# Two of the four block sums of a seven-product group move from VectorE to accumulating DMAs, and blocks take any free slot

## The chip, the cores and the metric

The kernel runs on one core of one Trainium2 chip. The metric is device time in microseconds (us) of one execution; the number for a kernel is the median of several runs. A profile is one more execution, recorded by the hardware profiler; its span runs from the first to the last instruction of the program.

## The reference, cut to what matters

One pre-norm decoder layer on 256 tokens of width 2048, with four token mixers side by side. Nearly all of the work is in products of 256 rows with wide float32 weights:

```python
h = rms_norm(x, norm_w)                      # 256 x 2048
p = h @ w_in                                 # 2048 x (z 2048, gates 8192, q/k/v of four mixers, indexer)
branches = (o_dsa, o_fox, o_diff, o_dil)     # four attentions, 4 heads of 128 each
for b in range(4):
    y = branches[b] * silu(z_parts[b])
    term = sigmoid(g_parts[b]) * (y @ w_branch[b])
    merged = term if merged is None else merged + term
out = rms_norm(x + merged @ w_out, final_norm_w)
```

## The kernel before

**Blocks, splits and products.** Weights come from HBM in blocks of 512 rows by 512 columns (1 MB, tile `raw`, 128 partitions x 2048 floats), each by one DMA of the SP queue. A block is cut in two halves of 128x1024. ScalarE copies each half to a rounded high part (`whi`, line 194), VectorE subtracts to get the low part (`wlo`, line 207), and TensorE multiplies in three passes: activation high by `whi`, activation low by `whi`, activation high by `wlo` (`three`, lines 365 to 367). There are 8 buffers for `whi` and 6 for `wlo`.

**Units.** The program is a list of units, each with one block and its matmuls. The main loop writes, for each half of each unit: the `wlo` split that lies 5 halves ahead, the `whi` split that lies 7 halves ahead, and then the matmuls of this half. What evicts a PSUM bank (`post`) is written after the unit's matmuls. The order of each engine's queue is the order in which this loop writes instructions; every engine works its queue in order and waits on semaphores.

**A group (`seven`).** A product of 256 tokens by 2048 rows by 1024 columns is a group of eleven units. For half of the rows the 2x2 blocks B11, B12, B21, B22 and the two halves of the tokens are combined so that seven products (P1 to P7, 12 matmuls each) take the place of eight. The other half of the rows goes through four plain units (c2a, c2b, c1a, c1b, 24 matmuls each). Four PSUM banks (X, Y, Z, W) collect. The seven products need four sums of blocks; before, all four are VectorE additions of whole blocks in place (`plus`, line 174). There are 17 groups: two (`ps_qk`, `ps_zv`) and two for the gates (`ps_g`) for each of the four mixers, and one for `w_out`. The usual order is P5 P1 P3 c2a P6 c2b P7 P2 c1a P4 c1b; the first group and the last one use another, written under `late`. P5 leaves its product in bank W. It is read from there (`p5`, by ScalarE), and c2a goes on adding to the same bank: for each half c2a has 6 matmuls to bank Z and then 6 to bank W.

**Slots.** There are six slots for `raw`. Before, each block has a fixed slot (0 to 3 for the B blocks, 4 and 5 for the others), and the next block of a slot is loaded when the last `wlo` split of the one before has been written.

**Threads.** Attention, the indexer and other small work are Python generators. A round of all active ones is written between units whenever a count of unit costs passes `pace`.

Of the kernel before, what the change touches and what calls it, by code (L numbers as in the profile page):

```python
# [20 lines left out]
KC = D // P  # L21
# [52 lines left out]
class Raw:  # L74


    def __init__(self, slot, src, k0, nk, c0, n):
        self.slot, self.src, self.k0, self.nk, self.c0, self.n = slot, src, k0, nk, c0, n
        self.tile = self.then = None
# [31 lines left out]
def body(ctx: ExitStack, tc, x, norm_w, w_in, fox_b_f, lq1, lk1, lq2, lk2, subln_w,  # L111
# [37 lines left out]
    waiting = [deque() for _ in range(SLOTS)]  # L149

    def load(r, parts=1, part=None):
        if not part:
            r.tile = wp.tile([P, 2048], F32, name="raw", tag=f"raw{r.slot}", bufs=1)
# [185 lines left out]
    def tok_units(src, c0, act, slots, evict, name, need=(), start=()):  # L339
# [3 lines left out]
        nk = 4 * len(slots)  # L343
        for i, slot in enumerate(slots):
# [5 lines left out]
            units.append(Unit(Raw(slot, src, 4 * i, 4, c0, 512), mm))  # L350
# [27 lines left out]
    def T_units(c0, evict, name, slots, ps_of=main_ps):  # L378
# [3 lines left out]
        for k0 in range(0, KC, 4):  # L382
# [11 lines left out]
            units.append(Unit(Raw(slots[k0 // 4], w_in, k0, 4, c0, 512), mm))  # L394
# [40 lines left out]
    def seven(src, c1, c2, base, ev, name, need={}, start=(), late=False, s0=0):  # L435
# [5 lines left out]
        B11, B12 = Raw(0, src, s0, 4, c1, 512), Raw(1, src, s0, 4, c2, 512)  # L441
        B21, B22 = Raw(3, src, s0 + 4, 4, c1, 512), Raw(2, src, s0 + 4, 4, c2, 512)
# [30 lines left out]
        def c(k0, c0, two):  # L473
            return Unit(Raw(4 + k0 // 4 % 2, src, k0, 4, c0, 512), plain(k0, two))
# [8 lines left out]
        def unit(what, raw, mm, post=(), frees=(), loads=(), pre=()):  # L483
            u = Unit(raw, mm, frees=frees, loads=loads, post=post, pre=pre, need=need.get(what, ()))
            u.cost = 12
            return u

        u5 = unit("P5", B12, product("V" if late else "W", form(1, 4), True),
                  [read(ev.p5, "V" if late else "W")], loads=[B12, B11, B22, B21],
                  pre=[lambda: plus(B12, B11)])  # L490
        u1 = unit("P1", B11, product("Y", whole(0, s0), True), [read(ev.p1, "Y")])
        u3 = unit("P3", B22, product("Z", form(0, 4), not late))
        second = [lambda: plus(B12, B22), lambda: free([B22])]
        fourth = [lambda: plus(B21, B12), lambda: free([B12])]
        u6 = unit("P6", B12, product("Y", form(0, 0)), [read(ev.u2, "Y")])
        u7 = unit("P7", B11, product("Y", form(1, 0)), [read(ev.u3, "Y")], frees=[B11],
                  pre=[lambda: plus(B11, B12, ALU.subtract)])
        u2 = unit("P2", B21, product("X", whole(0, s0 + 4), True))
        u4 = unit("P4", B21, product("Y", whole(1, s0 + 4)), frees=[B21])
        c2a, c2b = c(p0, c2, "ZW"), c(p0 + 4, c2, "ZW")  # L500
        c1a, c1b = c(p0, c1, "XY"), c(p0 + 4, c1, "XY")
        c2a.need += need.get("c2a", ())
        c1b.need += need.get("c1b", ())
        c1b.post += [read(ev.c11, "X", True), read(ev.c21, "Y", True)]
        c1b.start += start
        if late:
            u5.after += second[:1]
            u3.after += second[1:]
            u6.after += fourth
            u1.cost = u2.cost = 24  # L510
            u7.post += [read(ev.c12, "Z", True), read(ev.c22, "W", True)]
            return [c2a, u1, u2, u5, u3, u6, c2b, u7, c1a, u4, c1b]
        u6.pre += second
        u2.after += fourth
        c2b.post += [read(ev.c12, "Z", True)]
        u2.post += [read(ev.c22, "W", True)]
        return [u5, u1, u3, c2a, u6, c2b, u7, u2, c1a, u4, c1b]

    class Tok:


        def __init__(self, dst, s1, s2, late=False):
            self.dst, self.s1, self.s2, self.late = dst, s1, s2, late

        def p1(self, ps):
            if self.late:
                self.d1, self.d2 = self.dst()
            nc.scalar.activation(self.d1[:, 0], ps, AF.Copy, scale=self.s1[:, 0:1])

        def p5(self, ps):  # L530
            if self.late:
                nc.scalar.activation(self.d2[:, 1], ps, AF.Copy, scale=self.s2[:, 1:2])
            else:
                self.d1, self.d2 = self.dst()
# [7 lines left out]
        def u3(self, ps):  # L542
            if self.late:
                nc.vector.scalar_tensor_tensor(self.d2[:, 1], ps, self.s2[:, 1:2],  # L544
                                               self.d2[:, 1], op0=ALU.mult, op1=ALU.subtract)
            else:
# [733 lines left out]
```

## Time and profile before

| | |
|---|---|
| median of 3 runs | 1005.34 us (1004.07 to 1007.09) |
| the profiled execution's own time | 1004.6 us |
| its span | 1002.8 us |
| TensorE busy, of the span | 959.9 us, 96% |
| VectorE busy | 852.9 us, 85% |
| ScalarE busy | 626.3 us, 62% |
| GpSimd busy | 50.2 us, 5% |
| mean granted TensorE clock | 0.985 |

A busy time is the union of an engine's instructions. The profiled execution took 1.8 us more than its span. A row of the view of waits names the instruction that waited, the one that released it, the total in us, how often, and the longest.

### The profile page before, as it was taken

Reading aid. Unit: us, or ns where it says so; the run is one execution under the profiler, and the core shown is the slowest. Engines: PE = TensorE matmul, PEld = TensorE weight load, DVE = VectorE, ACT = ScalarE, POOL = GpSimd, SP = SyncE. Lnnn points to the kernel's source line nnn. Section 1 sums busy time; section 2 is a strip of 40 time slices with the busy share of each in tenths; the row PEclk is TensorE's granted clock in tenths of the full one; section 3 lists DMA queues with packets and bytes.
Section 4 is the critical chain, followed back from the end, with each engine's and each line's share of the span. In section 5 each row is a group of like instructions: output and inputs, shape, how many; then the busy total and the mean of one; then the engine's idle time right before and its main releaser. Section 6 shows DMA issues by size and latency. Waiting matters only on the chain.

```text
span 1002.8 us, 12075 instructions
## 1 busy us (share of the span) xinstructions
PE 959.9 (96%) x4443; PEld 790.4 (79%) x4443; DVE 852.9 (85%) x985; ACT 626.3 (62%) x828; POOL 50.2 (5%) x67
## 2 busy tenths in 40 slices
PE   9997898999999999889999999999999999999896
PEld 8876686878888887668888887788888878888676
DVE  5898899989788987789799899887998989779982
ACT  5847464796655656685456667864666787544551
POOL 2010000000000000020100000001000000010130
PEclk9999899999999999899999999999999999999998
DMA  9936355555766555337786655577756465866232
GB/s 318 298 134 196 124 168 167 169 168 184 278 225 228 197 168 168 126 126 238 223 232 202 218 168 168 168 262 208 236 201 210 164 210 187 309 232 238 86 125 84
DMA packets 100043, 195.81 MB, mean 195 GB/s; under 512 B 7811, under 2 KB 10021, under 8 KB 99600
## 3 DMA queue, kind: packets, MB, share of 16 engines
q1 hardware_dynamic: 96240, 181.06, 53.5%
q0 software_dynamic: 3712, 13.98, 5.3%
q8 instruction: 35, 0.57, 0.2%
q14 instruction: 24, 0.20, 0.1%
q10 hardware_dynamic: 32, 0.01, 0.0%
HBM read 186.61 MB, written 8.41 MB: 194 GB/s over the span
## 4 chain that ended last, share of the span: by engine, by line
PE 78%; DVE 13%; issue 4%; ACT 3%; DMA 1%; POOL 0%; ACTq 0%; POOLq 0%; DVEq 0%; SPq 0%
PE ps_g L365 9%; PE ps_g L367 9%; PE ps_g L366 9%; DVE wlo L207 6%; PE ps_zv L367 5%; PE ps_zv L365 5%; PE ps_zv L366 5%; PE ps_qk L365 5%; PE ps_qk L366 5%; PE ps_qk L367 5%; PE ps_iq L370 3%; PE ps_b L367 3%; PE ps_b L365 3%; PE ps_b L366 3%; DVE raw L174 3%
## 5 line engine op out<-in xcount | busy, mean ns | idle before, releaser
L194 ACT ACTIVATE whi<-raw 128x1024 fp32r<-128x1024 f32 (+1 forms) x439 | 448.1, 1051 | 221.3 <-DVE raw L174 70.1
L207 DVE TENSOR_TENSOR wlo<-raw,whi 128x1024 fp32r<-128x1024 f32 (+1 forms) x439 | 523.2, 1222 | 44.6 <-ACT whi L194 9.9
L174 DVE TENSOR_TENSOR raw<-raw 128x2048 f32<-128x2048 f32 x68 | 155.6, 2288 | 19.4 <-DMA raw<-in_w_in_dram 17.9
L365 PE MATMUL ps_g<-whi,hT 128*128 128x512 f32 x352 | 141.9, 403 | 0.0
L367 PE MATMUL ps_g<-wlo,hT 128*128 128x512 f32 x352 | 138.2, 393 | 0.0
L366 PE MATMUL ps_g<-whi,hT 128*128 128x512 f32 x352 | 138.1, 392 | 0.0
L365 PEld LDWEIGHTS ps_g<-whi,hT 128*128 128x128 f32 x352 | 66.7, 189 | 15.2 <-issue 1.6
L367 PEld LDWEIGHTS ps_g<-wlo,hT 128*128 128x128 f32 x352 | 66.7, 189 | 14.4
L366 PEld LDWEIGHTS ps_g<-whi,hT 128*128 128x128 f32 x352 | 66.7, 190 | 13.3
L365 PE MATMUL ps_qk<-whi,hT 128*128 128x512 f32 x176 | 69.8, 396 | 4.4 <-DVE tok L544 4.4
L367 PE MATMUL ps_zv<-wlo,hT 128*128 128x512 f32 x176 | 69.7, 396 | 3.0 <-DVE wlo L207 3.0
L365 PE MATMUL ps_zv<-whi,hT 128*128 128x512 f32 x176 | 69.7, 396 | 0.7 <-ACT v L547 0.7
L366 PE MATMUL ps_qk<-whi,hT 128*128 128x512 f32 x176 | 69.3, 394 | 0.0
L367 PE MATMUL ps_qk<-wlo,hT 128*128 128x512 f32 x176 | 69.2, 393 | 0.0
L366 PE MATMUL ps_zv<-whi,hT 128*128 128x512 f32 x176 | 69.0, 392 | 0.0
L365 PE MATMUL ps_g<-whi,sf 128*128 128x512 f32 x128 | 52.2, 408 | 0.0
L366 PE MATMUL ps_g<-whi,sf 128*128 128x512 f32 x128 | 50.3, 393 | 0.0
L367 PE MATMUL ps_g<-wlo,sf 128*128 128x512 f32 x128 | 50.3, 393 | 0.0
L365 PE MATMUL ps_b<-whi,yT 128*128 128x512 f32 x128 | 49.8, 389 | 0.0
L367 PE MATMUL ps_b<-wlo,yT 128*128 128x512 f32 x128 | 49.8, 389 | 0.0
L366 PE MATMUL ps_b<-whi,yT 128*128 128x512 f32 x128 | 49.8, 389 | 0.0
L365 PEld LDWEIGHTS ps_qk<-whi,hT 128*128 128x128 f32 x176 | 33.6, 191 | 12.4 <-DVE tok L544 4.8
(266 smaller groups left out, 1519.9 us busy)
## 6 DMA issues: line engine op xcount, KB each, us to landing
raw<-in_w_in_dram SPq DMA_DIRECT2D x132, 1024.0 KB, 5.1
raw<-in_w_branch_dram SPq DMA_DIRECT2D x16, 1024.0 KB, 5.3
raw<-in_w_out_dram SPq DMA_DIRECT2D x16, 1024.0 KB, 5.3
md<-g POOLq DMA_DIRECT2D x12, 512.0 KB, 5.3
raw<-in_w_in_dram SPq DMA_DIRECT2D x7, 512.0 KB, 9.7
xs<-in_x_dram SPq DMA_DIRECT2D x8, 256.0 KB, 7.5
mp<-md POOLq DMA_DIRECT2D x4, 512.0 KB, 3.6
xf<-in_x_dram POOLq DMA_DIRECT2D x2, 1024.0 KB, 7.8
```

Source lines behind the costliest of these rows:

```text
L174: nc.vector.tensor_tensor(to.tile, of.tile, to.tile, op=op)
L194: nc.scalar.activation(u.parts[0][h][:, s_], raw[:, s_], AF.Copy)
L207: nc.vector.tensor_tensor(u.parts[1][h][:, s_], raw[:, s_], u.parts[0][h][:, s_].bitcast(F32), op=ALU.subtract)
L365: nc.tensor.matmul(ps, ahi, u.hi(k)[:, cols], start=first, stop=False, skip_group_check=on)
L366: nc.tensor.matmul(ps, alo, u.hi(k)[:, cols], start=False, stop=False, skip_group_check=on)
L367: nc.tensor.matmul(ps, ahi, u.lo(k)[:, cols], start=False, stop=last, skip_group_check=on)
L370: nc.tensor.matmul(ps[:m], u.hi(k)[:, j * P:j * P + m], hT[:, k0 + k].rearrange("p a s -> p (a s)"), start=k0 + k == 0, stop=False)
```

## The change

- Sum 1, B12 + B11: before, VectorE (`plus(B12, B11)`). Now a DMA from GpSimd's queue reads B11 from HBM once more and adds it to B12 in its slot (`plus_dram`). It is written two units after B12's load.
- Sum 2, B12 + B22: stays on VectorE. It is written behind the `wlo` split of P5's second half.
- Sum 3: before, VectorE subtracted (`plus(B11, B12, SUBTRACT)`) in B11's slot. Now a DMA reads B12 from HBM once more and adds it to B22 in B22's slot, written right behind sum 2. P7 uses this block.
- Sum 4, B21 + B12: stays on VectorE.
- The usual order becomes P1 P3 P5 c2a P6 c2b P7 P2 c1a P4 c1b. The first group has P1 P2 P3 P5 c2a P6 c2b P7 c1a P4 c1b, the one of `w_out` c2a P1 P3 P5 c2b P6 P2 P7 c1a P4 c1b. Only that last group has P5 in a bank of its own (V); everywhere else P5 uses bank W, and c2a is the next unit.
- One queue of blocks in order of need (B12 four units early) in place of six; a freed slot goes to the next block.
- Attention threads begin after the group `ps_qk` in place of `ps_zv`, wait for their values (`ready`, `values`), and the costs and paces differ. The differential attention has one more round between its transposes and the product with the values.

The core of the diff:

```diff
+    def step_behind(only=None):
+        for item in list(behind):
+            item[0] -= 1
+            if item[0] <= 0 or item[1] is only:
+                behind.remove(item)
+                item[1].then()
...
         if r.then:
-            r.then()
+            behind.append([2, r])
 
     def free(raws):
         for r in raws:
-            if waiting[r.slot]:
-                load(waiting[r.slot].popleft())
+            slots.append(r.slot)
+            if waiting:
+                load(waiting.popleft())
...
-        B11, B12 = Raw(0, src, s0, 4, c1, 512), Raw(1, src, s0, 4, c2, 512)
-        B21, B22 = Raw(3, src, s0 + 4, 4, c1, 512), Raw(2, src, s0 + 4, 4, c2, 512)
+        order = order.split()
+        apart = order.index("c2a") < order.index("P5")
+        B11 = Raw(src, s0, 4, c1, 512)
+        B12 = Raw(src, s0, 4, c2, 512, lead=4)
+        B21, B22 = Raw(src, s0 + 4, 4, c1, 512), Raw(src, s0 + 4, 4, c2, 512)
+        B12.then = lambda: plus_dram(B12, B11)
...
+        Q = "V" if apart else "W"
...
+            "P5": Unit(B12, product(Q, form(1, 4), True), [read(ev.p5, Q)], frees=()),
...
+            "P7": Unit(B22, product("Y", form(1, 0)), [read(ev.u3, "Y")], frees=[B22], loads=()),
...
+        U["P5"].after.append(lambda: plus(B12, B22))
+        last_of("P3", "P5").after.append(lambda: plus_dram(B22, B12))
+        last_of("P2", "P6").after += [lambda: plus(B21, B12), lambda: free([B12])]
...
+        step_behind()
         for f in u.post:
             f()
```

How it moves instructions is seen in one group, `ps_zv` of the third mixer in the program's order. ScalarE's queue before, around the eviction of P5 (line 535, which reads bank W); raw_4247 is B12 + B11, raw_4223 is B22, raw_4330 the block of c2a:

```order
L194 ACTIVATE whi_4421<-raw_4282 128x1024 [waits DVE_49]
L194 ACTIVATE whi_4432<-raw_4247 128x1024 [waits DVE_49,PE_49,Activation_49]
L535 ACTIVATE v_4441<-ps_zv_4423,rst_109 128x512 [waits PE_49]
L194 ACTIVATE whi_4448<-raw_4247 128x1024 [waits Activation_49]
L194 ACTIVATE whi_4460<-raw_4330 128x1024 [waits DMAHW5_49,PE_49,Activation_49]
```

ScalarE's queue of the changed kernel around the same eviction (now line 539); raw_4246 is B22, and whi_4480 is the first half of P7's block, B22 + B12; DMASW2 is the semaphore of the DMA that makes this sum:

```order
L536 ACTIVATE tok_4439<-ps_zv_4422,rst_109 128x512 [waits DMASW5_49,PE_49]
L207 ACTIVATE whi_4448<-raw_4142 128x1024 [waits Activation_49]
L207 ACTIVATE whi_4459<-raw_4304 128x1024 [waits DMAHW4_49,PE_49,Activation_49]
L207 ACTIVATE whi_4469<-raw_4304 128x1024 [waits PE_49,Activation_49]
L207 ACTIVATE whi_4480<-raw_4246 128x1024 [waits DMASW2_49,PE_49,Activation_49]
L539 ACTIVATE v_4440<-ps_zv_4471,rst_109 128x512 [waits PE_49]
L610 ACTIVATE qk_4442<-turn_4490 128x512 [waits PE_49]
L207 ACTIVATE whi_4500<-raw_4246 128x1024 [waits Activation_49]
```

Before, the eviction of P5 stood between splits of P6's block, which wait for a VectorE sum. Now the split of the block that the second DMA makes stands directly ahead of it. The same two rows stand next to each other in all groups but that of `w_out`, 16 times.

TensorE's queue of the changed kernel, from the last matmuls of P5 (bank W is ps_zv_4471) to c2a's first ones in that bank (ps_zv_4450 is bank Z, turn_4490 the transposes of a thread):

```order
L380 MATMUL ps_zv_4471<-wlo_4416,sf_540 128x512
L608 MATMUL turn_4490<-ident_82,tok_4137 128x128 [waits PE_49]
L608 MATMUL turn_4490<-ident_82,tok_4137 128x128 [waits Activation_49]
L608 MATMUL turn_4490<-ident_82,tok_4137 128x128 x2
L378 MATMUL ps_zv_4450<-whi_4400,hT_105 128x512
L379 MATMUL ps_zv_4450<-whi_4400,hT_105 128x512
L380 MATMUL ps_zv_4450<-wlo_4429,hT_105 128x512 [waits DVE_49]
L378 MATMUL ps_zv_4450<-whi_4400,hT_105 128x512
L379 MATMUL ps_zv_4450<-whi_4400,hT_105 128x512
L380 MATMUL ps_zv_4450<-wlo_4429,hT_105 128x512
L378 MATMUL ps_zv_4471<-whi_4400,hT_105 128x512 [waits Activation_49]
```

The last row waits for the eviction of P5. Before, P5 was the group's first unit, and 24 matmuls of P1 and P3 and 6 of c2a stood between it and this row; now 6 of c2a do.

VectorE's and GpSimd's queues of the changed kernel at the second DMA: the splits of P5's block (raw_4142) with the sum behind them, and the DMAs, of which the second is sum 3 of this group:

```order
L220 TENSOR_TENSOR wlo_4398<-raw_4142,whi_4374 128x1024 [waits DVE_49,DMASW1_49,PE_49,Activation_49]
L561 SCALAR_TENSOR_TENSOR tok_4137<-ps_qk_4308,rsth_111,tok_4137 128x512 [waits DMASW3_49,PE_49]
L220 TENSOR_TENSOR wlo_4416<-raw_4142,whi_4384 128x1024 [waits DVE_49,PE_49,Activation_49]
L187 TENSOR_TENSOR raw_4142<-raw_4246,raw_4142 128x2048 [waits DVE_49]
L220 TENSOR_TENSOR wlo_4429<-raw_4281,whi_4400 128x1024 [waits DMAHW3_49,PE_49,Activation_49]
```

```order
L191 DMA raw_4142<-in_w_in_dram 128x4x512 [waits DMAHW5_49,DMAHW3_49,DMAHW7_49,DMASW1_49,DVE_49]
L191 DMA raw_4246<-in_w_in_dram 128x4x512 [waits DMASW2_49,DMAHW2_49,DVE_49,Activation_49]
L191 DMA raw_4446<-in_w_in_dram 128x4x512 [waits DMAHW3_49,DMAHW6_49,DMAHW1_49,DMAHW7_49,DMASW3_49,DVE_49]
```

Before, a group had four rows of the kind of the fourth one on VectorE and none of the DMAs; now it has two of each. wlo_4416 takes the buffer of the `wlo` written six places earlier, which the last unit of the group before (c1b) reads in its second half.

## Rows read from the trace of the kernel before

**Rows 1.** The page: span, busy time (share) of each engine, DMA queues.
```profile
span 1002.8 us, 12075 instructions
PE 959.9 (96%) x4443; PEld 790.4 (79%) x4443; DVE 852.9 (85%) x985; ACT 626.3 (62%) x828; POOL 50.2 (5%) x67
...
q1 hardware_dynamic: 96240, 181.06, 53.5%
q0 software_dynamic: 3712, 13.98, 5.3%
```

**Rows 2.** Waits of TensorE: waiter, releaser, total us, times, longest.
```profile
PE od L886 <- ACT pt L813: 8.0, 2, 4.0
PE o L855 <- ACT pt L813: 6.2, 5, 2.2
PE ps_qk L365 <- DVE tok L544: 4.4, 1, 4.4
PE ps_o L367 <- DVE wlo L207: 3.5, 3, 1.7
...
PE ps_zv L367 <- DVE wlo L207: 3.0, 2, 2.6
```

**Rows 3.** Groups by line: busy us, mean ns of one, idle before.
```profile
L207 DVE TENSOR_TENSOR wlo<-raw,whi 128x1024 fp32r<-128x1024 f32 (+1 forms) x439 | 523.2, 1222 | 44.6 <-ACT whi L194 9.9 <-issue 8.1 <-PE ps_zv L367 6.0
L194 ACT ACTIVATE whi<-raw 128x1024 fp32r<-128x1024 f32 (+1 forms) x439 | 448.1, 1051 | 221.3 <-DVE raw L174 70.1 <-PE ps_b L366 44.6 <-PE ps_qk L366 27.6
L174 DVE TENSOR_TENSOR raw<-raw 128x2048 f32<-128x2048 f32 x68 | 155.6, 2288 | 19.4 <-DMA raw<-in_w_in_dram 17.9 <-DVE wlo L207 0.9
```

**Rows 4.** Line 535, eviction of P5 by ScalarE: ns min/median/max.
```profile
L535 ACT ACTIVATE v<-ps_zv,rst x4: 690/690/691, 129.1 to 746.7; 128x512 f32<-128x512 f32 x4
```

**Rows 5.** Busy time in windows: us, each engine, clock, DMA share, GB/s.
```profile
300.00:330.00 30.00, 30.00 (x134) 24.83 (x133) 25.82 (x22) 16.17 (x16) 0.00 (x0) 1.00 0.67 226
```

**Rows 6.** The page, DMA issues: KB each, median us to landing.
```profile
raw<-in_w_in_dram SPq DMA_DIRECT2D x132, 1024.0 KB, 5.1
```

**Rows 7.** Tile md, window 274 to 292 us: stores of 512 KB without addition.
```profile
L962 POOL DMA_DIRECT2D md<-g x4: 534/545/564, 274.6 to 291.1; - x4
...
DMA to landing us min/median/max: 2.9/3.1/3.3
```

**Rows 8.** Tile md, window 489 to 510 us: stores of 512 KB that add.
```profile
L962 POOL DMA_DIRECT2D md<-g x4: 852/876/953, 489.5 to 506.0; - x4
...
DMA to landing us min/median/max: 5.3/5.5/6.2
```

**Rows 9.** Windows around one store that adds (500.30) and one that doesn't.
```profile
500.30:505.70 5.40, 5.40 (x26) 4.46 (x25) 5.40 (x6) 2.13 (x2) 0.85 (x1) 1.00 0.62 97
...
285.50:288.50 3.00, 3.00 (x15) 2.48 (x14) 3.00 (x3) 1.06 (x1) 0.53 (x1) 1.00 0.42 175
```

**Rows 10.** Issue of a 512-row and a 128-row DMA by GpSimd, ns.
```profile
L307 POOL DMA_DIRECT2D bias<-vdr x3: 770/816/820, 75.1 to 507.0; - x3
...
L307 POOL DMA_DIRECT2D mask<-vdr x1: 543/543/543, 75.9 to 75.9; - x1
```

**Rows 11.** Windows in and after four waits of TensorE, columns as in 5.
```profile
104.50:108.90 4.40, 0.01 (x1) 0.01 (x1) 4.33 (x8) 2.11 (x3) 0.00 (x0) 0.74 0.15 20
108.90:113.40 4.50, 4.50 (x11) 3.53 (x12) 4.43 (x10) 1.06 (x1) 0.54 (x1) 0.50 0.59 214
...
411.90:417.20 5.30, 5.30 (x14) 4.03 (x14) 4.55 (x6) 5.04 (x12) 0.15 (x1) 0.50 0.59 197
...
444.40:448.20 3.80, 3.79 (x13) 3.27 (x14) 3.80 (x5) 3.80 (x8) 0.77 (x1) 0.55 0.49 137
...
168.00:171.60 3.60, 3.58 (x9) 2.87 (x10) 3.60 (x4) 1.06 (x1) 0.00 (x0) 0.53 0.67 209
```

More of the change, by code (lines that the diff above doesn't have):

```diff
@@ L481, in read @@
             return g
[L483 to L517, printed above, removed]
+        def last_of(*names):
+            return U[max(names, key=order.index)]
+        Q = "V" if apart else "W"
+        U = {
+            "P1": Unit(B11, product("Y", whole(0, s0), True), [read(ev.p1, "Y")]),
+            "P2": Unit(B21, product("X", whole(0, s0 + 4), True), frees=()),
+            "P3": Unit(B22, product("Z", form(0, 4), not apart), frees=()),
+            "P4": Unit(B21, product("Y", whole(1, s0 + 4)), frees=[B21], loads=()),
+            "P5": Unit(B12, product(Q, form(1, 4), True), [read(ev.p5, Q)], frees=()),
+            "P6": Unit(B12, product("Y", form(0, 0)), [read(ev.u2, "Y")], frees=(), loads=()),
+            "P7": Unit(B22, product("Y", form(1, 0)), [read(ev.u3, "Y")], frees=[B22], loads=()),
+            "c2a": c(p0, c2, "ZW"), "c2b": c(p0 + 4, c2, "ZW"),
+            "c1a": c(p0, c1, "XY"), "c1b": c(p0 + 4, c1, "XY"),
+        }
@@ new lines, in seven @@
+        U["P5"].after.append(lambda: plus(B12, B22))
+        last_of("P3", "P5").after.append(lambda: plus_dram(B22, B12))
+        last_of("P2", "P6").after += [lambda: plus(B21, B12), lambda: free([B12])]
+        last_of("P3", "P6", "c2b").post.append(read(ev.c12, "Z", True))
+        last_of("P7", "c2b", "P2").post.append(read(ev.c22, "W", True))
+        U["c1b"].post += [read(ev.c11, "X", True), read(ev.c21, "Y", True)]
+        U["c1b"].start += start
+        for what, u in U.items():
+            u.need += need.get(what, ())
+            u.cost = 24 if s0 else 12
@@ L830, in put_y, with ready, values @@
         nc.vector.tensor_tensor(yT[:, h, 1], y, yT[:, h, 0].bitcast(F32), op=ALU.subtract)
+    def ready(b, h, early):
+        while any(a[0] in ("qk", "index", "fox", "const") for a in active):
+            yield
+        if h < early:
+            for _ in range(2 * h):
+                yield
+        else:
+            while V.get("v of") != b:
+                yield
+            for _ in range(h - early):
+                yield
+                yield
+    def values(b):
+        while V.get("v of") != b or any(a[0] == "z" for a in active):
+            yield
     def head_thread(b, h):
@@ L834, in head_thread @@
             V["yT"] = big.tile([P, 4, 2, S], F32R, name="yT", tag="y")
-        for _ in range(2 * h):
-            yield
+        yield from ready(b, h, 2)
         ps = att_ps("lps")
@@ L861, in diff_thread @@
             V["yT"] = big.tile([P, 4, 2, S], F32R, name="yT", tag="y")
-        for _ in range(2 * h):
-            yield
+        yield from ready(b, h, 1)
         er = []
@@ L1095, in mm @@
                 final(1, S, part)
-        units = [Unit(Raw(slots[i], w_out, 4 * i, 4, n * 512, 512), mm) for i in range(4)]
+        units = [Unit(Raw(w_out, 4 * i, 4, n * 512, 512), mm) for i in range(4)]
         units[-1].keep = True
@@ L1133, in body @@
     units[last_gate + 4].post.append(load_x_again)
-    units += out_units(2, (4, 5, 2, 1))
+    two = out_units(2)
     for n in range(4):
-        units[n - 4].need.append(f"merge{n}")
-    units += seven(w_out, 0, 512, lambda: V["mT"], Out(), "ps_o", late=True, s0=8,
-                   need={"P5": ["merge3"]})
+        two[n].need.append(f"merge{n}")
+    group = seven(w_out, 0, 512, lambda: V["mT"], Out(), "ps_o", s0=8, need={"P3": ["merge3"]},
+                  order="c2a P1 P3 P5 c2b P6 P2 P7 c1a P4 c1b")
+    units += two[:3] + group[:1] + two[3:] + group[1:]
     units[last_gate + 7].post.append(load_fw)
-    units += out_units(3, (2, 1, 0, 4))
+    units += out_units(3)
     warm = att_ps("warm")
@@ L1156, in body @@
         load(units[p_ // 2].raw, 2, p_ % 2)
-    for u in units[4:]:
-        for r in u.loads:
-            waiting[r.slot].append(r)
-    load(waiting[4].popleft())
-    load(waiting[5].popleft())
+    rest = [(i - r.lead, i, r) for i, u in enumerate(units) if i > 3 for r in u.loads]
+    waiting += [r for _, _, r in sorted(rest, key=lambda e: e[:2])]
+    load(waiting.popleft())
+    load(waiting.popleft())
     spin(WARM)
@@ L1218, in high @@
         if i < len(units):
+            if any(r is units[i].raw for _, r in behind):
+                step_behind(units[i].raw)
             split_hi(units[i], h, kept(units[i]))
```

76 lines of the change are left out of this document (38 added, 38 removed).

## The prediction

> **What bounds the kernel now.** I read the page first: TensorE is busy 959.9 of 1002.8 us, VectorE 852.9, the DMA engines 58.8% with both queues [rows 1]. So TensorE is the bound, and all that can be won lies in what it waits for. The view of its waits comes next [rows 2]. Two releasers carry it: ScalarE's copy of transposed probabilities (8.0 + 6.2 = 14.2 us) and VectorE (4.4 + 3.5 + 3.0 = 10.9 us), 25.1 us in all. VectorE is close behind TensorE, but its lateness reaches TensorE in few places, because up to six `wlo` halves lie between them. Behind the longer waits the clock is down: the one of 4.4 us, the two whose longest is 4.0 us and the one of 2.6 us are each followed by 3.6 to 5.3 us at a granted clock of 0.50 to 0.55 [rows 2, 11]. That is the lower of the two levels, 1.2 GHz. TensorE had stood idle just before.
>
> The measure for everything below is TensorE's pace where nothing holds it up: 134 matmuls in 30 us, 0.224 us each [rows 5]. P units (12 matmuls) take 2.69 us, c units (24) 5.37 us, a group 40.3 us.
>
> **What is removed.** 34 of 68 VectorE sums of 2.288 us, 77.8 us of VectorE's 852.9 [rows 1, 3]. TensorE gets from it at most what it waits for VectorE, 10.9 us. The threads' new spacing can win at most the other 14.2 us; in the order as much TensorE work stands as before. With the stretches at half clock behind those waits (4.5 us for 11 matmuls in place of 2.5, 5.3 for 14, 3.8 for 13, 3.6 for 9: 2.0, 2.2, 0.9 and 1.6 us, 6.7 us [rows 11]) the ceiling of the gain is 31.8 us, the floor nothing. I take 25, since both causes get clearly more room, but the waits of the first group come partly from the indexer, which stays.
>
> **What is added: 34 accumulating DMAs of 1 MB.** The trace has no such DMA into SBUF. The nearest rows are GpSimd's stores of 512 KB to HBM. Without addition they land in 2.9 to 3.3 us [rows 7], with addition in 5.3 to 6.2 us [rows 8]. In the window of one that ran beside no load the 16 engines were busy 0.62 x 5.4 = 3.35 us, in that of one without addition 0.42 x 3.0 = 1.26 us [rows 9]. Addition costs the engines 2.7 times as much. For 1 MB I add one more half at that price: 5.3 + 3.35 = 8.65 us. Our DMA has 512 rows of 2 KB in place of 128; the issue of 512 rows takes 0.82 us against 0.54 [rows 10], so 0.3 more: 8.9 us alone. A block load costs the engines 0.535 x 1002.8 / 181.06 x 1.05 = 3.1 us [rows 1], and in the order one is issued while the second DMA of a group runs. If all of it comes in between, 12 us. I take 9.2. The lower bound is addition into SBUF at the pace of a plain copy: 3.1 + 1.26 = 4.4 us [rows 7, 9]; a plain 1 MB load lands in 5.1 [rows 6].
>
> The Trainium skill ("DMA: Bandwidth & Descriptors", section "Anatomy of one DMA") gives a fit for GpSimd's DMAs, 2.0 us and the bytes at 436 GB/s, without a word on addition: 4.4 us for 1 MB, an estimate from that page, by which the change would come out as the first rival below. For 512 KB the fit gives 3.2 us: the trace agrees where nothing is added (3.1) and not where something is (5.5) [rows 7, 8].
>
> **Where that time falls: sum 3.** In 16 of 17 groups ScalarE's split of P7's first half, which waits for this DMA, stands directly ahead of the eviction of P5, and c2a's seventh matmul waits for that eviction. The DMA can't start early: it is behind sum 2, and that is behind the second `wlo` split of P5's block, whose buffer comes free when c1b of the group before is through, which is when P1 starts. So, from P1's start:
> - the work ahead of c2a's seventh matmul is P1, P3, P5 and 6 matmuls: 42 x 0.224 = 9.4 us, and about 0.4 us for threads' small matmuls such as the four transposes in the rows of the order (an estimate from the pace: 4 short ones, not more than 4 x 0.224 = 0.9): 9.8 us;
> - the chain is 1.22 (`wlo`) + 2.29 (sum 2) + the DMA + 1.05 (`whi`) + 0.69 (eviction) = 5.25 us and the DMA [rows 3, 4].
>
> The DMA has 9.8 - 5.25 = 4.55 us. Before, the same matmul had P1 and P3 (5.4 us) between itself and P5, and no DMA ahead of it. With 9.2 us TensorE waits 4.65 us in each of 16 groups: 74 us. No row shows the hand-overs by semaphore; I set them to nothing, and they only add. A VectorE that is late at that place adds as well. While ScalarE stands, later splits stand behind it, but they are 7 halves ahead of TensorE (over 10 us), so they are not late in their turn; behind the eviction nothing new is late.
>
> A wait of this size costs clock too. By the four stretches above, 1.7 us each: 27 us.
>
> **What I cost at nothing.**
> - Sum 1, the other 17 DMAs: B12's load is written in P3 of the group before, and its split in P4, some 29 us of TensorE's work later. Load (5.1), a possible wait behind sum 3's DMA (9.2) and the DMA (9.2) make 23.5. Cover 5 us; if it goes, ScalarE stands as long as the excess.
> - Slots: counted along the new order, the shortest time from a slot's release to its block's first split is some 12 us (B11) against 5.1 for a load; before, the shortest was some 8 us.
> - GpSimd's queue: 34 issues of about 1.2 us on an engine that is busy 5% [rows 1]. The stores of `md` and two small operations of the differential attention stand behind DMAs that wait for a load; nobody needs them within a unit.
> - The group of `w_out`: P5 has a bank of its own, so c2b doesn't wait; P7's split has over 12 us before TensorE needs it.
> - DMA engines: 34 x 6.7 = 228 us more on 590 us makes 818 of some 1080 us, 76%. Not the bound.
>
> **The sum.** 74 + 27 - 25 = +76 us on the profiled execution's 1004.6 us (span 1002.8 and 1.8 around it; 0.7 under the median): 1080.6, say 1080 us.
>
> **The rivals.**
> - *Faster.* The DMA adds at a plain copy's pace, 4.4 us. Then it fits the 4.55 us, nothing waits, and the gain of 25 stays: 980 us. For it: no row shows addition into SBUF. Against it: rows 8 and 9. The point that decides is a landing of 4.55 us; at 6.1 us, 16 x 1.55 = 25 us eat the gain.
> - *No change.* A landing near 6.1 us, with waits too short to lower the clock: 1005 us. It needs a landing in a narrow band, between a plain load's and the doubled one's.
> - *Slower still.* The added 228 us of engine time meet the loads, so that the DMA takes 12 us: 16 x 7.45 = 119, 2.0 x 16 = 32 for clock, gain 20: +131, 1136 us. For it: a share of 0.67 in a plain stretch before [rows 5]. Against it: only one load falls into the window in the order.
>
> **How the numbers follow.** My case has 70%, with landings of 8.0 to 10.5 us: waits of 3.45 to 5.95 us (55 to 95 us), clock 16 to 32, gain 32 to 15, so +39 to +112, 1044 to 1117 us; that is the likeliest one's own range. Slower still has 7%, no change 6%, faster 17%. Slower by over 0.3% (3 us, about what this kernel's runs can tell apart) is 0.77. No change holds some results either side of 0.3%, so same is 0.05 and faster 0.18. The range of eight in ten must reach into the faster case: 982 to 1115.
>
> **What would show it.** Right: a row of TensorE waiting for ScalarE's line 539 in c2a, some 16 times 4 to 5 us; ScalarE's `whi` waiting for `raw` from HBM on GpSimd's queue; landings of 9 us; stretches at 0.5 clock after each. Busy time of VectorE down by 78 us. Wrong: landings under 5 us, or TensorE's waits at that matmul under 1 us each. The forecast fails most simply through the landing: each microsecond of it is worth 16 us.

## The result and the profile after

The changed kernel takes 1119.87 us (1117.46 to 1121.87 in 3 runs), against 1005.34: the ratio is 1.1136, 95% interval 1.1092 to 1.118. The forecast was 1080 us with a range up to 1115. Direction and mechanism came out as forecast; the loss is 115 us in place of 76, and the range was left by 4.9 us.

The page of the changed kernel: span, busy times, the queue that GpSimd feeds, and its 1 MB DMAs with their median landing; they answer to [rows 1].

```profile
span 1117.9 us, 12163 instructions
...
PE 989.6 (89%) x4443; PEld 811.8 (73%) x4443; DVE 788.8 (71%) x950; ACT 635.1 (57%) x834; POOL 91.7 (8%) x101
...
q1 hardware_dynamic: 96240, 181.06, 46.8%
q0 software_dynamic: 21664, 49.63, 23.5%
...
raw<-in_w_in_dram POOLq DMA_DIRECT2D x32, 1024.0 KB, 9.9
```

The same 4443 matmuls keep TensorE busy for 29.7 us more (989.6 against 959.9), which is a lower clock (0.937 over the span against 0.985). Its idle time went from 42.9 to 128.3 us, 85.4 more. Together that is the 115.1 us by which the span is longer. VectorE is 64 us less busy, where 78 were forecast (the sums alone take 76.7 less), and the time shows nothing of it. The view of TensorE's waits answers to [rows 2]:

```profile
PE ps_g L378 <- ACT g L539: 36.0, 6, 9.1
PE ps_qk L378 <- ACT tok L539: 34.0, 4, 10.0
PE ps_zv L378 <- ACT v L539: 24.6, 4, 6.2
PE o L875 <- ACT pt L815: 14.6, 4, 6.7
PE ps_qk L380 <- DVE wlo L220: 4.4, 3, 2.0
PE ps_o L378 <- DVE xf L1061: 2.9, 2, 2.0
PE ps_g L380 <- DVE wlo L220: 2.7, 2, 2.3
```

The first three rows are the predicted one: c2a's seventh matmul waits for the eviction of P5, 14 times, 94.6 us, 6.76 us each in the mean. One such group, `ps_zv` of the third mixer in the program's order, on the timeline. The columns are start, duration, engine, instruction, and the idle time before it with its releaser:

```profile
357.70 0.39 PE L378 MATMUL ps_zv<-whi,hT 128*128 128x512 f32 x1
...
357.96 1.22 DVE L220 TENSOR_TENSOR wlo<-raw,whi 128x1024 fp32r<-128x1024 f32 x1 [0.67 <-PE ps_qk L380]
359.21 2.29 DVE L187 TENSOR_TENSOR raw<-raw 128x2048 f32<-128x2048 f32 x1
...
362.22 1.28 POOL L191 DMA_DIRECT2D raw<-in_w_in_dram  x1 [36.22 <-DVE raw L187]
...
372.17 1.06 ACT L207 ACTIVATE whi<-raw 128x1024 fp32r<-128x1024 f32 x1 [6.07 <-DMA raw<-in_w_in_dram]
373.13 0.67 ACT L539 ACTIVATE v<-ps_zv,rst 128x512 f32<-128x512 f32 x1
...
373.85 0.79 PE L378 MATMUL ps_zv<-whi,hT 128*128 128x512 f32 x1 [5.99 <-ACT v L539]
```

It is to be read downwards as one chain: P1 starts as the last matmul of the group before releases a `wlo` buffer, the split, sum 2, the DMA of sum 3, the split of its result, the eviction behind it in ScalarE's queue, TensorE. Times to landing (min/median/max) of all 34 accumulating DMAs, and then of the one issued at 184.9, the one above, and the one at 555.1:

```profile
DMA to landing us min/median/max: 8.3/9.9/13.1
...
DMA to landing us min/median/max: 8.3/8.3/8.3
...
DMA to landing us min/median/max: 9.8/9.8/9.8
...
DMA to landing us min/median/max: 12.8/12.8/12.8
```

In the trace the 16 of sum 3 that stand ahead of an eviction take 8.35 to 12.79 us, 9.75 in the mean (worked out over the 16). At 184.9 no load comes in for the first 5.9 us of the DMA; in the group above one begins 1.6 us after it. The windows over the work, the wait and what follows, columns as in [rows 5]:

```profile
357.70:367.88 10.18, 10.16 (x47) 8.09 (x45) 9.89 (x8) 6.12 (x7) 1.28 (x1) 1.00 0.38 62
367.88:373.88 6.00, 0.03 (x1) 0.03 (x1) 0.44 (x1) 1.71 (x3) 0.00 (x0) 0.92 1.07 321
373.85:379.88 6.03, 6.03 (x14) 4.74 (x15) 1.23 (x1) 2.44 (x3) 1.28 (x1) 0.51 0.89 200
...
379.88:383.00 3.12, 3.12 (x17) 2.58 (x16) 1.33 (x2) 1.54 (x3) 0.00 (x0) 1.00 0.79 143
```

During the wait the DMA share is printed as 1.07. A share over 1 can't be exact; it is read here as engines that are busy for about all of the wait. Behind it 14 matmuls take 6.03 us at a granted clock of 0.51, the 1.2 GHz level, in place of 14 x 0.224 = 3.14 [rows 5]; then the clock is back at 1.00. So this wait costs 2.9 us of clock, where [rows 11] gave 1.7. Over the 14 waits the trace has 156 such matmuls at the low level, at 0.427 us each in place of 0.224: some 32 us (an estimate from these rows).

### The profile page after: what moved, and what is told of

Its sections match the earlier page's. It is cut to its first block, busy times and chain, and to the rows that moved or that the text cites. A ratio compares the mean times of both kernels' runs of the same rounds, so it can differ in the third digit from the quotient of the medians.

```text
span 1117.9 us, 12163 instructions
## 1 busy us (share of the span) xinstructions
PE 989.6 (89%) x4443; PEld 811.8 (73%) x4443; DVE 788.8 (71%) x950; ACT 635.1 (57%) x834; POOL 91.7 (8%) x101
## 3 DMA queue, kind: packets, MB, share of 16 engines
q1 hardware_dynamic: 96240, 181.06, 46.8%
q0 software_dynamic: 21664, 49.63, 23.5%
## 4 chain that ended last, share of the span: by engine, by line
PE 42%; DMA 6%; DVE 4%; issue 2%; ACT 2%; POOLq 0%; ACTq 0%; POOL 0%; DVEq 0%
DMA raw<-in_w_in_dram 6%; PE ps_g L378 5%; PE ps_g L379 5%; PE ps_g L380 5%; PE ps_zv L378 2%; PE ps_qk L378 2%; PE ps_zv L379 2%; PE ps_zv L380 2%; PE ps_qk L379 2%; PE ps_qk L380 2%; PE ps_b L380 2%; PE ps_b L378 2%; PE ps_b L379 2%; DVE wlo L220 2%; PE ps_o L378 2%
## 5 line engine op out<-in xcount | busy, mean ns | idle before, releaser
L378 PE MATMUL ps_g<-whi,hT 128*128 128x512 f32 x352 | 145.7, 414 | 36.0 <-ACT g L539 36.0
L379 PE MATMUL ps_g<-whi,hT 128*128 128x512 f32 x352 | 141.8, 403 | 0.0
L380 PE MATMUL ps_g<-wlo,hT 128*128 128x512 f32 x352 | 141.3, 401 | 0.3 <-DVE wlo L220 0.3
L378 PEld LDWEIGHTS ps_g<-whi,hT 128*128 128x128 f32 x352 | 69.3, 197 | 54.3 <-ACT g L539 38.5
L378 PE MATMUL ps_qk<-whi,hT 128*128 128x512 f32 x176 | 73.0, 415 | 34.0 <-ACT tok L539 34.0
L378 PE MATMUL ps_zv<-whi,hT 128*128 128x512 f32 x176 | 75.2, 427 | 24.6 <-ACT v L539 24.6
L191 POOL DMA_DIRECT2D raw<-in_w_in_dram x32 | 41.9, 1308 | 660.9 <-DVE raw L187 434.1
L187 DVE TENSOR_TENSOR raw<-raw 128x2048 f32<-128x2048 f32 x34 | 78.9, 2320 | 1.1
L379 PEld LDWEIGHTS ps_g<-whi,hT 128*128 128x128 f32 x352 | 69.3, 197 | 13.8
L379 PE MATMUL ps_zv<-whi,hT 128*128 128x512 f32 x176 | 72.6, 412 | 0.0
L380 PE MATMUL ps_zv<-wlo,hT 128*128 128x512 f32 x176 | 72.3, 411 | 0.0
L379 PE MATMUL ps_qk<-whi,hT 128*128 128x512 f32 x176 | 71.8, 408 | 0.0
L378 PEld LDWEIGHTS ps_zv<-whi,hT 128*128 128x128 f32 x176 | 35.6, 202 | 33.9 <-ACT v L539 26.3
L378 PE MATMUL ps_b<-whi,yT 128*128 128x512 f32 x128 | 49.9, 390 | 0.0
```

The lines of the kernel that those rows point to most:

```text
L187: nc.vector.tensor_tensor(to.tile, of.tile, to.tile, op=op)
L191: nc.gpsimd.dma_start(to.tile.rearrange("p (k n) -> p k n", k=of.nk), of.src[of.k0 * P:(of.k0 + of.nk) * P, of.c0:of.c0 + of.n] .rearrange ...
L378: nc.tensor.matmul(ps, ahi, u.hi(k)[:, cols], start=first, stop=False, skip_group_check=on)
L379: nc.tensor.matmul(ps, alo, u.hi(k)[:, cols], start=False, stop=False, skip_group_check=on)
L380: nc.tensor.matmul(ps, ahi, u.lo(k)[:, cols], start=False, stop=last, skip_group_check=on)
```

## The experiments

The theory: sum 3's DMA stands ahead of P5's eviction in ScalarE's queue, and P5 directly ahead of c2a, so that TensorE waits for the DMA. Rivals: the DMA engines' time, sum 1's DMA, and the new scheme of the threads. Each run is compared with runs of the kernel before on the same chip. Except where it is said, the edits are to the changed kernel.

**Eviction ahead of the split.** P5's `post` is written before the split of the block that the DMA makes (`evict_first` is set for P5 in all groups but that of `w_out`); the DMAs stay.

```diff
-            high(2 * i + h + HI - 1)
-            u.mm(u, h)
+            if h and u.evict_first:
+                u.mm(u, h)
+                for f in u.post:
+                    f()
+                high(2 * i + h + HI - 1)
+            else:
+                high(2 * i + h + HI - 1)
+                u.mm(u, h)
...
-        for f in u.post:
-            f()
+        if not u.evict_first:
+            for f in u.post:
+                f()
```

> The queue theory (ScalarE's eviction of P5 stands behind the split that waits for sum 3's DMA, and TensorE's c2a waits for that eviction): the DMAs stay as they are, only the eviction of P5 is written ahead of that split. The 14 waits of TensorE for line 539 (94.6 us) go to under 0.5 us each, with most of the stretches at half clock behind them; 970 to 1000 us. ScalarE still waits some 9 us for the DMA in every group. The rival (the DMAs' added engine time, 23.5% of the span on GpSimd's queue, slows the block loads, whatever stands where): nothing of this changes, 1090 to 1120 us.

Measured: 1023.52 us, ratio 1.0175 (1.016 to 1.019). With all 34 DMAs running, 96 of the 115 us are back, some 23 of them TensorE's busy time (966.9 us in place of 989.6). So the order in ScalarE's queue carries most of the loss, and the engines' time does not. But 970 to 1000 was missed. The waits that are left, in this kernel's view of waits:

```profile
PE o L877 <- ACT pt L817: 14.6, 4, 6.7
PE ps_g L379 <- ACT g L541: 14.1, 5, 3.7
```

The second row is the eviction again, now without a DMA ahead of it: six matmuls are too little cover when ScalarE is at something else. Ahead of one of these waits it was at a thread's sigmoid (`sg`) and a split:

```profile
595.81 1.06 ACT L626 ACTIVATE sg<-tok 128x1024 f32<-128x1024 f32 x1
596.77 1.04 ACT L208 ACTIVATE whi<-raw 128x1024 fp32r<-128x1024 f32 x1
...
598.44 0.50 PE L379 MATMUL ps_g<-whi,hT 128*128 128x512 f32 x1 [3.37 <-ACT g L541]
```

The first row above is the threads' (below).

**The same DMA without addition.** Sum 3's DMA overwrites B22 with B12, so P7's block isn't the sum.

```diff
-    def plus_dram(to, of):
+    def plus_dram(to, of, op=ALU.add):
...
-                            .rearrange("(k p) n -> p k n", p=P), accum_op=ALU.add)
+                            .rearrange("(k p) n -> p k n", p=P), accum_op=op)
...
-        last_of("P3", "P5").after.append(lambda: plus_dram(B22, B12))
+        last_of("P3", "P5").after.append(lambda: plus_dram(B22, B12, ALU.bypass))
```

> Sum 3's DMA copies in place of adding (so P7 gets B12 alone and the output is not the reference's). The queue theory: landing falls from 9.8 us to about 5.2, that of a plain load, each wait of TensorE from 6.7 to about 2.2 us, and little is left of the half-clock stretches: 1025 to 1045 us. The rival (engine time): 17 x (6.7 - 2.7) = 68 us less for the 16 engines, which are busy 70% of the span and wait for nobody most of the time: above 1095 us.

Measured: 1053.8 us, 1.0484 (1.0465 to 1.0503), 9 us above the upper end of 1025 to 1045, and far from the rival's 1095. The DMA of the group shown above, the row of the four `ps_zv` groups, the split and the matmul of that group, and GpSimd's DMA queue on the page:

```profile
DMA to landing us min/median/max: 5.8/5.8/5.8
...
PE ps_zv L378 <- ACT v L539: 6.7, 4, 1.9
...
342.63 1.06 ACT L207 ACTIVATE whi<-raw 128x1024 fp32r<-128x1024 f32 x1 [2.00 <-DMA raw<-in_w_in_dram]
...
344.32 0.79 PE L378 MATMUL ps_zv<-whi,hT 128*128 128x512 f32 x1 [1.93 <-ACT v L539]
...
q0 software_dynamic: 17312, 49.63, 20.1%
```

So addition costs this DMA 4.0 us (9.8 against 5.8). The copy also moves the same bytes in fewer packets, 17312 against 21664, which is 256 fewer for each of the 17 DMAs; no run separates what the addition costs from what the smaller packets cost.

Over the 16 the mean landing falls from 9.75 to 5.73 and the time by some 66 us, 16 us for each microsecond. That the forecast has the same number is in part luck: its 16 were waits alone, and of these 51.6 us went (94.6 to 43.0), 12.8 for each; the rest is clock. The 43.0 us that stay are of two kinds. Before nine of the 14 waits, 28.7 us, the split still waits for the shorter DMA, as in the group shown; before the other five, some 14 us, it starts without a wait, and the eviction stands behind ScalarE's own work.

The Trainium skill ("Collectives: The Full Stack", section "The bandwidth ceiling: the fold count and why AG ≠ RS ≠ AR") puts the price of a reduction in the DMA engines down to its two source reads, a ratio of 1.93 there. Here the landings stand as 1.7 to 1, and the engines' time as some 2 to 1 (an estimate from the shares of GpSimd's queue: (0.235 x 1117.9 - 0.053 x 1002.8) / 34 = 6.2 us for a DMA that adds, and (0.235 x 1117.9 - 0.201 x 1048.7) / 17 = 3.1 us less without). That is near the page's ratio, but no run here separates the two reads.

**Half of the rows.** Sum 3's DMA adds only the first 256 of 512 rows; the other half of P7's block is left without its sum.

```diff
+    def plus_dram(to, of, nk=4):
...
+        nc.gpsimd.dma_start(to.tile.rearrange("p (k n) -> p k n", k=of.nk)[:, :nk],
+                            of.src[of.k0 * P:(of.k0 + nk) * P, of.c0:of.c0 + of.n]
...
-        last_of("P3", "P5").after.append(lambda: plus_dram(B22, B12))
+        last_of("P3", "P5").after.append(lambda: plus_dram(B22, B12, 2))
```

> Sum 3's DMA adds only the first half of the block's rows (512 KB; P7 gets the other half without its sum, so the output is not the reference's). The queue theory: a landing of about 5.5 us, as the stores of 512 KB that add, so waits of about 2.5 us: 1030 to 1050 us, near the run that doesn't add. If the wait came from the number of DMAs or their issue and not from their length, it would stay near 1110 us.

Measured: 1061.89 us, 1.0533 (1.0484 to 1.0581), 12 us above the expected band. From this kernel's page:

```profile
raw<-in_w_in_dram POOLq DMA_DIRECT2D x16, 512.0 KB, 5.9
```

Half the bytes with addition land about as late as all of them without, and the times are near each other. TensorE pays for the length of the landing, whatever makes it. Of the 45.4 us of waits for line 539 that stay here, 31.4 us (ten waits of 14) still have a split that waits for the DMA ahead of them; the others don't, as in the run before.

**Sum 3 back on VectorE**, in B11's slot as before; sum 1 stays a DMA.

```diff
-            "P7": Unit(B22, product("Y", form(1, 0)), ..., frees=[B22], loads=()),
+            "P7": Unit(B11, product("Y", form(1, 0)), ..., frees=[B11], loads=()),
-        last_of("P3", "P5").after.append(lambda: plus_dram(B22, B12))
+        last_of("P3", "P5").after.append(lambda: free([B22]))
+        U["P7"].pre.append(lambda: plus(B11, B12, ALU.subtract))
```

> Sum 3 back on VectorE, in B11's slot as before; sum 1 stays a DMA, and orders, slots and threads stay as changed. The queue theory: no DMA ahead of the eviction of P5, TensorE waits for it under 1 us each: 970 to 1000 us. The rival that the new unit order, the free slots or the threads' spacing cost the time: still above 1080 us.

Measured: 1043.78 us, 1.0374 (1.0359 to 1.039). My 970 to 1000 fell: without this DMA the changed order still loses some 38 us. The same rows stand in its view of waits:

```profile
PE ps_g L378 <- ACT g L540: 25.9, 6, 6.5
...
PE ps_qk L378 <- ACT tok L540: 6.8, 4, 3.9
...
180.09 1.06 ACT L207 ACTIVATE whi<-raw 128x1024 fp32r<-128x1024 f32 x1 [1.89 <-DVE raw L187]
```

A VectorE sum ahead of the eviction makes TensorE wait as well, if there are only six matmuls between P5 and its bank's next use. The third row shows it for the group whose eviction starts at 181.06; TensorE waits 5.1 us there. But that is so in two of the 11 waits, 10.2 of 33.2 us: before the others the split directly ahead of the eviction starts without a wait, behind other work of ScalarE.

**Both sums on VectorE**: as the last one, and sum 1 as well (`U[...].pre.append(lambda: plus(B12, B11))`, with a lead of 2 in place of 4).

> The changed kernel with sums 1 and 3 both on VectorE again; order of units, slots and threads as changed. If sum 3's DMA behind the eviction of P5 and the place of P5 directly ahead of c2a are the two causes, then nearly nothing changes against the kernel with sum 3 alone on VectorE (1043.8): 1035 to 1050 us, the rows of TensorE waiting for the eviction still some 30 us in all. Rival, the DMA of sum 1 (with its load and its engines' time) costs something of its own: below 1030 us.

Measured: 1045.88 us, 1.0396 (1.0376 to 1.0416), as the theory said. With and without sum 1's DMA the intervals overlap: no cost of that DMA can be told here.

**Only the threads undone.** Starts, waits, costs, paces and rounds are those of the kernel before.

```diff
-        while any(a[0] in ("qk", "index", "fox", "const") for a in active):
+        for _ in range(2 * h):
             yield
-        if h < early: ...
     def values(b):
-        while V.get("v of") != b or any(a[0] == "z" for a in active):
-            yield
+        yield from ()
...
-                      start=[("qk", qk_thread)] + start, ...
+                      start=[("qk", qk_thread)], ...
-                        "ps_zv", need={"c1b": ["qk"]}, start=[("z", z_thread)]))
+                        "ps_zv", need={"c1b": ["qk", "fox", "const"] + ...}, start=[z_thread] + start))
```

> The changed kernel with nothing but the threads undone (starts, waits, costs, paces and rounds of before); P5 stands directly ahead of c2a, its eviction behind the split that waits for sum 3's DMA. If my theory holds, all 16 waits at c2a stay, now also in the two groups where a wait for pt took their place: 90 to 105 us of waits for line 539, 1090 to 1110 us. Rival, the threads make a large part of the 114 us: below 1080 us.

Measured: 1119.21 us, 1.1121 (1.1098 to 1.1144): no difference to the changed kernel, 9 us above my band. Its waits for line 539:

```profile
PE ps_g L378 <- ACT g L539: 40.7, 8, 9.2
PE ps_qk L378 <- ACT tok L539: 34.7, 4, 10.2
PE ps_zv L378 <- ACT v L539: 24.2, 4, 6.3
```

All 16 are there now, 99.6 us. The two groups without one in the changed kernel had the threads' wait of 6.7 us for `pt` in its place. Either is hidden behind the other.

**Eviction ahead of the split, and the threads undone**: the first edit and the last one together.

> The kernel with P5's eviction written ahead of the split, and the attention threads with their starts, waits, costs and paces of the kernel before. If the new threads' scheme is what is left to pay there (fourth head waiting for an lg buffer, bursts of probabilities for TensorE), the two waits of 6.7 us for pt go, and some of the 14 us behind P5's eviction: 1000 to 1012 us against 1023.5. Rival, what is left comes from P5 standing directly ahead of c2a, with only 6 matmuls to cover the eviction: 1018 to 1026 us, and the waits at c2a stay at 14 us or more.

Measured: 1010.17 us, 1.0053 (1.0036 to 1.0069), in the theory's band. The two rows of 6.7 us for `pt` are gone; 16.0 us of waits for P5's eviction stay, one of them 8.2. So the threads' scheme costs some 12 us (1.0175 to 1.0053), but only where the DMA's wait doesn't cover it.

What it does is seen in the changed kernel's timeline ahead of 719, where TensorE's wait is not the DMA's:

```profile
708.41 0.29 DVE L797 TENSOR_TENSOR lg<-lps,bias 128x128 f32<-128x128 f32 x1 [10.61 <-PE ptp L813]
...
710.12 1.28 ACT L804 ACT_TABLE_LOAD   x1 [10.17 <-DVE mx L802]
...
718.60 0.86 ACT L815 ACTIVATE pt<-ptp 128x384 f32<-128x384 f32 x2
...
719.14 1.22 PE L875 MATMUL o<-pt,v 128*128 128x256 f32 x2 [6.72 <-ACT pt L815]
```

A head's logits on VectorE wait 10.6 us for transposes (`ptp`) that read an earlier head's `lg`; there are three `lg` buffers. VectorE stands in its queue, ScalarE behind it, and then everything comes at once. That the heads hold their buffers because they wait for the values (`values`) was argued from the code and tried only together with the rest of the scheme.

**P5 first.** The order becomes P5 P1 P3 c2a ..., sum 2 and sum 3's DMA stand behind P3; both DMAs, the slots and the changed threads stay, and the first group keeps its order.

```diff
-              order="P1 P3 P5 c2a P6 c2b P7 P2 c1a P4 c1b", s0=0):
+              order="P5 P1 P3 c2a P6 c2b P7 P2 c1a P4 c1b", s0=0):
-        U["P5"].after.append(lambda: plus(B12, B22))
+        last_of("P3", "P5").after.append(lambda: plus(B12, B22))
```

> The changed kernel with P5 as the first unit in the usual order (P5 P1 P3 c2a ...), sum 2 and the DMA of sum 3 behind the later of P5 and P3; both DMAs, slots and threads stay as changed. If the place of P5 is the whole matter, TensorE has P1 and P3 (5.4 us) more for the eviction, the eviction stands ahead of the split that waits for the DMA, and what is left are the threads' waits (some 15 us) and the first group's, which keeps its order (10 us and its clock): 1020 to 1035 us, one row of TensorE waiting for the eviction in place of 14. Rival, the engines' time of the 34 DMAs holds up loads wherever the sums stand: over 1060 us, with waits for raw in all groups.

Measured: 1030.55 us, 1.0262 (1.0235 to 1.0289), as the theory said. Of the waits for P5's eviction one is left, the first group's, and the threads' stay:

```profile
PE o L878 <- ACT pt L818: 15.2, 4, 6.7
PE ps_qk L378 <- ACT tok L542: 9.8, 1, 9.8
PE ps_qk L378 <- DVE tok L546: 8.1, 2, 7.0
```

**P5 first, threads undone**, and in the first group the eviction ahead of the split (the edits above).

> As the kernel with P5 first, and in addition the threads as before and in the first group P5's eviction ahead of the split. If order and threads are all that the change costs, both DMAs remain, VectorE is 65 to 78 us less busy than before, and the waits for VectorE go: 985 to 1003 us, faster than the kernel before. Rival, VectorE's 78 us were never on the path, and the DMAs cost a little: 1004 to 1015 us.

Measured: 1007.73 us, 1.0032 (1.0021 to 1.0043). The rival's band held: all that could be seen as a loss is repaired, and still nothing is won. The 7.0 us in the third row above are a new wait, and it is still there. Its place in this kernel:

```profile
714.13 1.31 POOL L192 DMA_DIRECT2D raw<-in_w_in_dram  x1 [8.70 <-issue]
714.90 1.11 POOL L711 DMA_DIRECT2D ncb<-ncd  x1
...
724.06 0.35 DVE L718 SCALAR_TENSOR_TENSOR sc<-ncb,cumc,mask 128x128 f32<-128x128 f32 x1 [7.83 <-DMA ncb<-ncd]
...
727.89 0.77 PE L379 MATMUL ps_qk<-whi,sf 128*128 128x512 f32 x1 [6.75 <-DVE tok L548]
```

The forgetting attention's bias (`ncb`) is loaded by GpSimd's queue too. It stands there behind a DMA of sum 1, ahead of which GpSimd was idle for 8.7 us with no releaser named; VectorE waits for `ncb`, and the eviction that TensorE needs stands behind that in VectorE's queue.

**That load on ScalarE's queue**: `nc.scalar.dma_start(ncb, ...)` for `nc.gpsimd.dma_start(ncb, ...)`.

> The kernel with P5 first and the threads as before, and the load of ncb (the forgetting attention's bias) issued from ScalarE's queue in place of GpSimd's. There it stood behind a DMA of sum 3 that waited 8.7 us, VectorE waited 7.8 us for it, and TensorE 6.75 us for VectorE, with 3 us of clock behind. If GpSimd's queue is the cause, the row of 6.75 us goes: 996 to 1002 us, faster than the kernel before. Rival, VectorE is late there for its own work or the load takes as long on any queue: 1004 to 1009 us.

Measured: 1004.71 us, 0.9988 (0.9978 to 0.9998). The load is issued at 705.3 in place of 714.9 and lands in 5.5 us; the row goes down:

```profile
PE ps_qk L379 <- DVE tok L548: 3.7, 3, 1.8
```

So the expected wait went, but the time is 0.4% lower where I had expected 0.6 to 1.2%. (The expectation called the DMA ahead of `ncb` one of sum 3. The DMA before that one, at 704.13, was released by VectorE's sum and so is sum 3's; the one at 714.13, ahead of `ncb`, is then sum 1's of the next group.)

**And one more round** between the transposes and the product with the values in the differential attention, one `yield`, which the change had as well.

> The last one, and in addition the one more round of the differential attention between its transposes and the product with the values, which the change had. If that round gives ScalarE's copies the time that TensorE waited (two rows of 4.0 and 3.1 us, and clock), 985 to 995 us. Rival, the copies are late for another reason, or the round moves the wait to another place: no difference to the last one.

Measured: 1000.45 us, 0.9949 (0.993 to 0.9968), faster than both kernels, if 5 us above my band. The waits for `od`, 7.0 us in the last kernel, are down to 0.8, and the longest rows in this one are others, with short waits:

```profile
PE ps_o L379 <- DVE xf L1056: 4.7, 2, 2.5
...
PE od L902 <- ACT pt L820: 0.8, 2, 0.6
```

**P5 first, threads undone, sums 1 and 3 on VectorE**: the kernel of 1007.73 us without its DMAs.

> The kernel with P5 first and the threads as before, with sums 1 and 3 on VectorE again: of the change only the slots are left, and the first group's order. If VectorE's 78 us are hidden behind TensorE wherever the order is right, this is as fast as the one with the DMAs or faster, since nothing of GpSimd's queue stands ahead of ncb: 998 to 1008 us. Rival, the DMAs do relieve the path: 1010 to 1025 us here.

Measured: 1009.49 us, 1.0039 (1.0026 to 1.0052), between the bands. The kernel with the DMAs has 1.0021 to 1.0043. So as long as `ncb` stands behind the DMAs, they bring nothing that can be told.

**The kernel of 1000.45 us with sums 1 and 3 on VectorE.**

> As the kernel of 1000.45 us (P5 first, threads as before, load of ncb by ScalarE's queue, one more round in the differential attention), with sums 1 and 3 on VectorE. If the two DMAs are worth something once nothing waits for them, VectorE has 75 us more to do and its lateness reaches TensorE: 1003 to 1009 us. Rival, all of the gain comes from the queue and the round: 998 to 1002 us.

Measured: 1007.34 us, 1.0014 (1.0002 to 1.0025), against 0.993 to 0.9968 with the DMAs, inside the first band. So once nothing waits for them, the two DMAs are worth 0.65%, some 6.5 us.

**The kernel before with the one round.**

> The kernel before with only the one more round of the differential attention. If the round takes away the two waits of 4.0 us and their clock by itself, 993 to 1000 us, and the DMAs are not needed for that. Rival, VectorE at 85% has no room, and the wait moves: 1003 to 1007 us.

Measured: 1000.68 us, 0.9952 (0.9933 to 0.997), 0.7 us above the band of 993 to 1000. One line in the kernel before is worth as much as all of the above. The DMAs in the kernel before's own order of the first group, with the round, were not tried.

## Why the prediction was wrong, by its own steps

**The path was right.** TensorE waits for line 539 at c2a's seventh matmul, `whi` waits for GpSimd's DMA, and the clock is at 0.50 behind it. Put the eviction ahead of the split, and 96 us are back. Three terms of the sum were mis-sized: +74 of waits, +27 of clock, -25 of gain. Measured are 94.6 of waits and 20.5 for the other two together (29.7 more of busy TensorE, 9.2 less of other idle time); with some 32 of clock behind the 14 waits, some 11 are left for the gain.

**74 us of waits: 94.6.** In the group shown, the step was 9.2 + 5.25 - 9.8 = 4.65. Measured there from P1's start (357.70) to TensorE's matmul (373.85) are 16.15 us, of which the DMA takes 9.84 and the rest of the chain 6.31; TensorE's own work is 16.15 - 5.99 = 10.16.
- The DMA: 9.8 and, in the mean, 9.75, for 9.2. Alone it was put at 8.9 and takes 8.35; a load beside it costs more than I took.
- The chain around it: 6.31 for 5.25. "I set them to nothing, and they only add" was the step that failed here: sum 2's end (361.50) to the DMA's issue (362.22) is 0.72, and P1's start to the split 0.26, which is 0.98 of the 1.06 missing.
- The work ahead: 10.16 for 9.8.

That "no row shows the hand-overs by semaphore" was not so. In the trace of the kernel before, VectorE's `g` ends at 489.06, and the store that waits for it is issued 0.44 us later:

```profile
488.37 0.69 DVE L960 TENSOR_TENSOR g<-ps_b,g 128x512 f32<-128x512 f32 x1 [0.67 <-PE ps_b L367]
...
489.50 0.95 POOL L962 DMA_DIRECT2D md<-g  x1 [39.53 <-DVE g L960]
```

So 5.99 for 4.65. The same group of the run without addition bears the sum out: 5.78 + 6.31 - 10.16 = 1.93, the wait that its timeline shows. Fourteen groups of that size give 83.9 us; three waits of 9.1 to 10.0 us add 11.1 more, 95.0 for the 94.6 measured. "A VectorE that is late at that place adds as well" is two of them (the first group, and the one at 493, where sum 2 came late); the third is the landing of 12.8 at 555. Two of 16 groups have no such wait; there `pt` holds TensorE for 6.7 us, as the run with the threads undone shows.

**25 us of gain: some 11.** The forecast took most of the 25.1 us of waits [rows 2]. Of these hardly any went: those for VectorE were 10.9 and are 10.0 (4.4 + 2.9 + 2.7), those for `pt` were 14.2 and are 14.6, in other places. That "both causes get clearly more room" was wrong of the threads, whose new waits make VectorE and ScalarE stand and then hurry. The 9.2 us by which the other idle time fell came mostly from rows that the sum had not counted: the indexer's (`ps_ix`), 4.9 us before, are not in the view any more. And VectorE's 78 us were of little use: taken away in an order where nothing waits, they bring 6.5 us.

**27 us of clock: some 32.** It was right in kind. The price for each wait was too low, 1.7 us where the wait shown costs 2.9 and the 14 some 2.3 in the mean; that it was put on 16 waits in place of 14 made up for part of that, by luck. One of the windows in [rows 11], 411.90 to 417.20, begins too late: TensorE is busy without a pause from 410.00 on, and from there to 417.20 the clock is 0.53. All in all TensorE's busy time rose by 29.7 us.

**What was costed at nothing.** Sum 1's DMA: right. The DMA engines: forecast 818 us of work, measured (0.468 + 0.235) x 1117.9 = 786; with the order mended no cost of them can be told, though they are busy for about all of the wait shown. GpSimd's queue: in the changed kernel right, with P5 first wrong by 6.75 us and its clock; "nobody needs them within a unit" had passed over `ncb`.

**The rivals.** *Faster* needed a landing of 4.55 us: even without addition it is 5.8. *Slower still* (12 us, 1136 us) had the right sign and the wrong cause: one landing of the 16 took that long. My own case ended at 1117 us: it let the landing vary, but left the hand-overs and VectorE's lateness, of which it said that they only add, at nothing. Its landings (8.0 to 10.5 us) hold the mean of 9.75, and its upper ends of waits (95) and clock (32) are about what was measured; its least gain, 15, is more than came. With waits and clock at those upper ends, it was the missing gain that took the result beyond 1117.

**What stays open.** Of the 38 us that the changed order loses without any DMA in sum 3's place, some 12 are the threads' where the eviction stands ahead; the parts of ScalarE's other work and of VectorE's lateness in the rest were not separated.

## What to carry to other kernels

Before a sum moves from an engine to a DMA, look at what stands behind the first reader of its result in that reader's queue: here an eviction that had nothing to do with the sum stood behind a landing of 9.75 us in each group, and writing it one place earlier gave 96 us back. Give the hand-overs and the latenesses of such a chain a value from the trace, if a rough one; at nothing they left out about 1 us in each group, some 15 us over the 14 waits, and the range was left by 4.9. An engine at 85% that reaches the bound by only 11 us of waits is worth about that much, however much work is taken from it; the cheapest gain was in the other row of the waits, one round of a thread.

## What the runs showed of the hardware

- A DMA from HBM that adds 1 MB into SBUF landed in 8.35 us where no load began in its first 5.9 us, and in 9.8 where a 1 MB load began 1.6 us into it; in the same place without addition in 5.8; 512 KB with addition in 5.9 (median).
- From VectorE's last write to the start of GpSimd's issue that waits for it were 0.72 us in the group shown; the issue itself takes 1.28 us there, and 0.77 in the run without addition.
- A small broadcast load behind such a DMA on GpSimd's queue landed in 9.1 us (8.5 in the kernel before, with no such DMA ahead), and in 5.5 us from ScalarE's queue, where it was issued 9.6 us earlier; the runs don't separate the queue from what else the engines moved at the time.
